# Attention branch with five seven-product quads in each pass, and one right factor formed ahead

## The chip, the cores and the metric

The kernel runs on one core of a Trainium2 chip. Its engines each work through an own stream of instructions: TensorE (PE: matmuls, and PEld: the loads of the stationary operand), VectorE (DVE), ScalarE (ACT), GpSimd (POOL), and SyncE (SP), which here only issues transfers. Sixteen DMA engines move data between HBM and the core's memory (SBUF). The metric is the device time of one launch in microseconds; the median of several runs is given, and a profile shows one execution in detail.

## What is computed

One layer that mixes dilated attention with a state-space scan, for 256 rows of width 2048, in float32. Cut to what matters here:

```python
hn = rms_norm(x, norm_w)
q, k, v, z_a, z_s, xbc, dt_raw, g_a, g_s = split(hn @ w_in)
...
o_a = o_a.reshape(b, s, ATTN_WIDTH) * silu(z_a)
y = rms_norm(y * silu(z_s), ssm_norm_w)
merged = sigmoid(g_a) * (o_a @ w_attn_branch) + sigmoid(g_s) * (y @ w_ssm_branch)
return rms_norm(x + merged @ w_out, final_norm_w)
```

The part that is changed is `o_a @ w_attn_branch`, a product of 256x2048 by 2048x2048 ("the attention branch").

## The kernel before

**Weights and units.** All weights lie in HBM as `wall`, an array of units of 128x1024 floats (512 KB), in the order in which they are used; `FIRST` gives each matrix's first unit. `load` (L263) fetches a unit into one of five tiles of a ring (`stream`, tag `w`, `W_BUFS = 5`). Float32 products are made from split operands: `unit` (L269) lets ScalarE round a unit to `h` (L278) and VectorE form the rest `l = w - h` (L279), each in one of four tiles (`H_BUFS = 4`). A product is then a triple of matmuls (`triple`, L483): left-high by h, left-high by l, left-low by h, lines L484 to L486.

**Stages, in order of time.** Scan stage (groups of the state-space part, with the x and z_s projections), the SSM branch, v, a loop over 16 heads (`q`, `k`, `za` projections, scores, mix), the attention gates `ga`, the attention branch `attn`, the output product `out`. The planner orders the instructions of each engine by a simulated timeline and by priorities; the order of the transfers on SP's queue comes with it.

**Passes and quads.** The products ga, attn and out run as two passes of 1024 columns each (c = 0 and c = 2), in `gemm_pair` (L469). A pass goes through eight quads; a quad is two blocks of 128 rows of the weights by two half-widths of 512 columns, for two halves of the 256 rows of the left side. A plain quad takes 2 x 2 x 2 products. A quad listed in `S_QUADS` takes seven, by Winograd's form of Strassen's product: it loads the four blocks of the weights (`wa` holds b11 and b21, unit n + 1 holds b12 and b22), forms T (two half-widths, from `b12 - b11` and `b22 - that`) and U = `wa` minus T's right half, splits four right factors (`ha/la`, `hc/lc`, `ht/lt`, `hu/lu`, by `part`, L550), and multiplies them with left factors; four of these are sums of blocks of the left side (`turn_x`, L450), made once and kept for both passes. The products that are shared go to four banks of their own (`prods`); `fold` (L585) adds them up at the end of a pass, and `attend` (L1146) then adds the plain sums and merges with the gates (L1143, L1144).

**Work done ahead.** T is formed ahead of time for the quads in `SUMS_ATT`: `sum_jobs` (L244) hangs a `get` behind a unit of the loop over the heads (two loads to a place in `th_a`, each behind a one-column copy on POOL, L249 and L250), and an `add` three units later (`SUM_LAG`): two half-width subtractions on VectorE (L254, L255) into a result place that itself waits for a POOL copy (L253), and a `spill` (L242) of 512 KB to HBM. The job frames are the same in the scan stage (`SUMS_SSM`). In the pass, T is loaded back (L533) along with b22 (L534); where `room` names places for these they take no tile of the ring. The left factors of o are made in `mix` behind every second head (`keep_left`, L425), spilled, and fetched on POOL's queue behind units named by `O_BEHIND` (L1115), into one buffer of the pool `xk` and four of `xl`, which until then hold the left factors of x.

**The branch before.** `S_QUADS` has (2, 4, 6) for pass 0 and (2, 4, 5, 6) for pass 2; the passes' orders of quads are in `A_ORDERS` (L41).

Of the kernel before, what the change touches and what calls it, by code (L numbers as in the profile page):

```python
# [24 lines left out]
UNIT = 1024  # L25
# [14 lines left out]
GS_BEFORE = {0: (0, 1), 4: (2,)}  # L40
A_ORDERS = {0: (0, 1, 2, 4, 3, 6, 5, 7), 2: (0, 2, 1, 4, 3, 5, 6, 7)}  # L41
V_ORDERS = {0: (0, 2, 4, 1, 3, 5, 6, 7), 2: (0, 2, 1, 4, 3, 5, 6, 7)}
# [9 lines left out]
    ("v", 0): (2, 3, 4, 5, 6), ("v", 2): (2, 4, 5, 6), ("ga", 0): (2, 3, 4, 5, 6), ("ga", 2): (2, 3, 4, 5, 6),  # L52
    ("attn", 0): (2, 4, 6), ("attn", 2): (2, 4, 5, 6), ("out", 0): (3, 5), ("out", 2): (3, 5),
}
# [4 lines left out]
SX_X = (2, 4, 3, 5, 6)  # L59
O_BEHIND = 3, 14, 15, 17  # L60
SUMS_ATT = [(t, q) for t in [(n, c) for n in ("ga", "attn", "out") for c in (0, 2)] for q in S_QUADS[t]]
ATT_QUADS = sorted({*S_QUADS[("attn", 0)], *S_QUADS[("attn", 2)]})
IN_PLACE = {"ssm": [(0, 12), (2, 12)]}
# [3 lines left out]
SUM_LAG = 3  # L67
# [58 lines left out]
FIRST = {}  # L126
# [72 lines left out]
def hybrid_block(ctx: ExitStack, tc: tile.TileContext, wall, xt, x, pk_d, cst_d, fw_d, out):  # L199
    nc = tc.nc  # L200
# [29 lines left out]
    on_unit = {}  # L230
    presum, lefts = {}, {}
    ssm_pool = []

    def behind_unit(n, f):
        on_unit.setdefault(n, []).append(f)
# [4 lines left out]
    def spill(kept, key, name, src, shape):  # L240
        kept[key] = dram.tile([P, *shape], F32, name=name, tag=name)
        nc.sync.dma_start(kept[key], src)  # L242

    def sum_jobs(jobs, units, places):  # L244

        def get(tag, q, t, b11, behind):
            n = FIRST[tag] + 2 * q
            for dst, src in ((t, wall[n + 1]), (b11, wall[n, :, :512])):
                gp.tensor_copy(dst[:, 0:1], behind)  # L249
                nc.sync.dma_start(dst, src)  # L250

        def add(tag, q, t, b11, res, behind):
            gp.tensor_copy(res[:, 0:1], behind)  # L253
            ve.tensor_tensor(res[:, :512], t[:, :512], b11, ALU.subtract)  # L254
            ve.tensor_tensor(res[:, 512:], t[:, 512:], res[:, :512], ALU.subtract)  # L255
            spill(presum, (tag, q), f"t_{tag[0]}{tag[1]}_{q}", res, [UNIT])

        for n, ((tag, q), u) in enumerate(zip(jobs, units)):
            t, b11, res = places[n % len(places)]
            behind_unit(u, lambda behind, a=(tag, q, t, b11): get(*a, behind))  # L260
            behind_unit(u + SUM_LAG, lambda behind, a=(tag, q, t, b11, res): add(*a, behind))

# [206 lines left out]
    def gemm_pair(tag, x_of, n_kt, sxs, swap, extra={}, close=1, order=None, room={}, tail=None):  # L469
# [22 lines left out]
        for at, q in enumerate(order):  # L492
# [29 lines left out]
            def place(kind):  # L522
                if not room.get(kind):
                    t = ring(f"{kind}{n}")
                    return t[:, 512:] if kind == "wc" else t
                seats[kind] = seats.get(kind, -1) + 1
                return room[kind][seats[kind] % len(room[kind])]

            wa = ring(f"wa{n}")
            nc.sync.dma_start(wa, wall[n])  # L530
            if made:
                wt, wc = place("wt"), place("wc")
                nc.sync.dma_start(wt, presum[tag, q])  # L533
                nc.sync.dma_start(wc, wall[n + 1, :, 512:])  # L534
            else:
                wt = ring(f"wb{n}")
                wc = wt[:, 512:]
                nc.sync.dma_start(wt, wall[n + 1])

            def hl(where, suffix, tags, bufs):  # L540
# [14 lines left out]
            with tc.high_priority(L_AHEAD):  # L555
                if not made:
                    ve.tensor_tensor(wt[:, :512], wt[:, :512], wa[:, :512], ALU.subtract)
                ha, la = hl(stream, "a", "hl", H_BUFS)
                part(wa, ha, la)
                hc, lc = hl(stream, "c", "hl", H_BUFS)  # L560
                part(wc, hc[:, :512], lc[:, :512])
                if not made:
                    ve.tensor_tensor(wt[:, 512:], wt[:, 512:], wt[:, :512], ALU.subtract)
                t2 = wt[:, 512:].unsqueeze(1).to_broadcast([P, 2, 512])
                ve.tensor_tensor(two(wa), two(wa), t2, ALU.subtract)
                ht, lt = pair_of("t")
                part(wt, ht, lt)
                hu, lu = pair_of("u")
                part(wa, hu, lu)
            sx = sxs[q]  # L570
# [121 lines left out]
    with tc.tile_pool(name="ssm", bufs=2) as sp:  # L692
# [212 lines left out]
        for c in GS_BEFORE[0]:  # L905
# [6 lines left out]
            SUMS_SSM, [FIRST[("B", g)] + n for g in range(1, 7) for n in SUM_UNITS],  # L912
            [(sums_at[:, 0], sums_at[:, 2, :512], sums_at[:, 1])],
        )
# [129 lines left out]
    with tc.tile_pool(name="att", bufs=2) as ap:  # L1044
# [33 lines left out]
        def mix(h, pT, za):  # L1078
# [204 lines left out]
```

## Time and profile before

| | |
|---|---|
| median of 3 runs | 1381.36 us (1379.6 to 1382.22) |
| the profiled execution | 1379.87 us, its span 1378.0 us |
| HBM read, written | 316.97 MB, 29.82 MB |
| loop over the heads | about 820 to 1115 us |
| attention gates | about 1116 to 1202 us |
| attention branch | 1196.8 to 1284 us |
| output product and end | from there to 1378 us |

A line of the groups names the source line, the engine, the operation, what is written from what (buffer numbers left out), the shape, the count, then busy time, mean ns of one, and the idle time in front of them with what ended it. A line of the waits names who waited for whom, the microseconds in total, how often, and the longest. A line of the stretches has its bounds, its length, the busy time of PE, PEld, DVE, ACT and POOL with counts, the granted clock, the DMA engines' busy share, and GB/s. A line of the DMA issues ends with the median microseconds from issue to landing. The stages overlap a little, since the planner lets matmuls of neighbouring quads interleave.

### The profile page before, as it was taken

Reading aid. Unit: us, or ns where it says so; the run is one execution under the profiler, and the core shown is the slowest. Engines: PE = TensorE matmul, PEld = TensorE weight load, DVE = VectorE, ACT = ScalarE, POOL = GpSimd, SP = SyncE. Lnnn points to the kernel's source line nnn. Section 1 sums busy time; section 2 is a strip of 40 time slices with the busy share of each in tenths; the row PEclk is TensorE's granted clock in tenths of the full one; section 3 lists DMA queues with packets and bytes.
Section 4 is the critical chain, followed back from the end, with each engine's and each line's share of the span. In section 5 each row is a group of like instructions: output and inputs, shape, how many; then the busy total and the mean of one; then the engine's idle time right before and its main releaser. Section 6 shows DMA issues by size and latency. Waiting matters only on the chain.

```text
span 1378.0 us, 20734 instructions
## 1 busy us (share of the span) xinstructions
PE 1366.8 (99%) x7260; PEld 1164.8 (85%) x7260; DVE 1177.0 (85%) x1763; ACT 840.0 (61%) x1310; POOL 161.7 (12%) x238
## 2 busy tenths in 40 slices
PE   9999999999999999999999999999999999999997
PEld 7888888888888888888888888888888888888886
DVE  6898899898899888788989888777877789988897
ACT  7655777675667676666565554454444557655564
POOL 2301211101020100010001001211211000400112
PEclk9999999999999999999999999999999999999999
DMA  9767878778787867578677568888889757875773
GB/s 342 237 190 237 298 267 286 262 244 288 248 277 237 298 203 220 174 242 277 228 261 270 211 215 316 306 275 280 306 298 302 230 163 267 291 244 173 246 273 122
DMA packets 106520, 348.15 MB, mean 253 GB/s; under 512 B 11888, under 2 KB 14256, under 8 KB 106416
## 3 DMA queue, kind: packets, MB, share of 16 engines
q1 hardware_dynamic: 104400, 340.67, 74.0%
q10 hardware_dynamic: 1440, 4.06, 0.8%
q0 software_dynamic: 576, 2.10, 0.4%
q8 instruction: 57, 0.93, 0.3%
q14 instruction: 47, 0.39, 0.1%
HBM read 316.97 MB, written 29.82 MB: 252 GB/s over the span
## 4 chain that ended last, share of the span: by engine, by line
PE 98%; DMA 0%; DVE 0%; ACT 0%; issue 0%; SPq 0%; POOL 0%; POOLq 0%; DVEq 0%
PE ps_xs L333 8%; PE ps_zs L333 8%; PE ps_k L333 4%; PE ps_za L333 4%; PE ps_q L333 4%; PE ps_zs L339 4%; PE ps_xs L339 4%; PE ps_ssm L485 3%; PE ps_ssm L486 3%; PE ps_ssm L484 3%; PE ps_q L339 2%; PE ps_za L339 2%; PE ps_k L339 2%; PE ps_gs L421 2%; PE ps_gs L422 2%; PE ps_gs L420 2%
## 5 line engine op out<-in xcount | busy, mean ns | idle before, releaser
L278 ACT ACTIVATE h<-w 128x1024 fp32r<-128x1024 f32 (+1 forms) x394 | 410.0, 1048 | 306.0 <-issue 73.7
L279 DVE TENSOR_TENSOR l<-w,h 128x1024 fp32r<-128x1024 f32 (+1 forms) x394 | 474.0, 1209 | 111.1 <-ACT h L278 106.9
L333 PE MATMUL ps_zs<-XT,h 128*128 128x512 f32 x496 | 172.0, 393 | 0.0
L333 PE MATMUL ps_xs<-XT,h 128*128 128x512 f32 x496 | 171.6, 393 | 0.0
L339 PE MATMUL ps_zs<-XT,l 128*128 128x256 f32 x496 | 134.6, 279 | 0.0
L339 PE MATMUL ps_xs<-XT,l 128*128 128x256 f32 x496 | 133.7, 277 | 0.0
L333 PEld LDWEIGHTS ps_xs<-XT,h 128*128 128x128 f32 x496 | 91.3, 188 | 19.4
L333 PEld LDWEIGHTS ps_zs<-XT,h 128*128 128x128 f32 x496 | 91.3, 188 | 18.9
L339 PEld LDWEIGHTS ps_zs<-XT,l 128*128 128x128 f32 x496 | 93.3, 188 | 2.1
L339 PEld LDWEIGHTS ps_xs<-XT,l 128*128 128x128 f32 x496 | 93.2, 188 | 2.1
L333 PE MATMUL ps_q<-XT,h 128*128 128x512 f32 x256 | 91.1, 404 | 0.0
L333 PE MATMUL ps_k<-XT,h 128*128 128x512 f32 x256 | 88.6, 395 | 0.0
L333 PE MATMUL ps_za<-XT,h 128*128 128x512 f32 x256 | 88.4, 394 | 0.0
L551 ACT ACTIVATE ha<-wa 128x1024 fp32r<-128x1024 f32 x45 | 47.5, 1056 | 45.9 <-PE ps_ssm L486 10.0
L339 PE MATMUL ps_q<-XT,l 128*128 128x256 f32 x256 | 68.4, 278 | 0.0
L339 PE MATMUL ps_k<-XT,l 128*128 128x256 f32 x256 | 68.4, 277 | 0.0
L339 PE MATMUL ps_za<-XT,l 128*128 128x256 f32 x256 | 68.4, 277 | 0.0
L552 DVE TENSOR_TENSOR la<-wa,ha 128x1024 fp32r<-128x1024 f32 x45 | 54.8, 1218 | 8.4 <-ACT ha L551 8.3
L552 DVE TENSOR_TENSOR ltu<-wa,htu 128x1024 fp32r<-128x1024 f32 x40 | 48.7, 1219 | 10.8 <-ACT htu L551 10.8
L793 ACT ACTIVATE gt<-acb,acT 128x128 f32<-128x128 f32 x128 | 44.1, 390 | 22.2 <-DMA acb<-acum_d 21.9
L333 PEld LDWEIGHTS ps_k<-XT,h 128*128 128x128 f32 x256 | 47.0, 188 | 9.9
L333 PEld LDWEIGHTS ps_q<-XT,h 128*128 128x128 f32 x256 | 47.1, 188 | 9.7
(691 smaller groups left out, 3347.8 us busy)
## 6 DMA issues: line engine op xcount, KB each, us to landing
w<-in_wall SPq DMA_DIRECT2D x390, 512.0 KB, 4.8
wa<-in_wall SPq DMA_DIRECT2D x45, 512.0 KB, 4.7
th_a<-in_wall SPq DMA_DIRECT2D x21, 512.0 KB, 4.7
sums_at<-in_wall SPq DMA_DIRECT2D x18, 512.0 KB, 5.0
acb<-acum_d SPq DMA_DIRECT2D x32, 256.0 KB, 3.8
t_ssm<-sums_at SPq DMA_DIRECT2D x13, 512.0 KB, 4.3
wt<-t_ssm SPq DMA_DIRECT2D x13, 512.0 KB, 4.7
th_a<-in_wall SPq DMA_DIRECT2D x21, 256.0 KB, 5.4
```

The source lines that it names most:

```text
L278: ac.activation(h[:, a:b], w[:, a:b], AF.Copy)
L279: ve.tensor_tensor(l[:, a:b], w[:, a:b], h[:, a:b].bitcast(F32), ALU.subtract)
L333: high = pe.matmul(acc, h[:, kk, :], xs_of(kt), start=(kt == 0), stop=False)
L339: low = pe.matmul(acc[:, S:], l[:, kk, :], xs_of(kt)[:, :S], start=False, stop=(kt == KT - 1))
L420: pe.matmul(accs[i], xh, h[:, kk], start=(kt == 0), stop=False)
L421: pe.matmul(accs[i], xh, l[:, kk], start=False, stop=False)
L484: pe.matmul(acc, xh, h, start=start, stop=False)
L485: pe.matmul(acc, xh, l, start=False, stop=False)
L486: pe.matmul(acc, xl, h, start=False, stop=stop)
L551: ac.activation(h, src, AF.Copy)
L552: ve.tensor_tensor(l, src, h.bitcast(F32), ALU.subtract)
L793: ac.activation(g4[:, n, b], acb[:, j, b // 2 * P : b // 2 * P + P], AF.Relu, scale=-1.0, bias=sc[:, h : h + 1],)
```

## The change

Both passes of the branch get the same five seven-product quads, 2 to 6, and the same order. A fifth left factor of o (quad 3) is made, spilled and fetched. For quads 3 to 6 of both passes U is formed ahead too: the job loads all of `wa`, forms T in place of its second operand, then U in place of `wa`, and spills both; in the pass U is loaded by a transfer of its own (alternately to a new tile `room_u` and to a tile of the ring) and `wa` stays as it is. Jobs now work in place, with no third place and no POOL copy at the add; the scan stage's jobs use two places by turns instead of one. There are 24 jobs in the loop over the heads in place of 21, spaced 17/5 units in place of 15/4.

```diff
-A_ORDERS = {0: (0, 1, 2, 4, 3, 6, 5, 7), 2: (0, 2, 1, 4, 3, 5, 6, 7)}
+A_ORDERS = {0: (0, 2, 3, 1, 4, 5, 6, 7), 2: (0, 2, 3, 1, 4, 5, 6, 7)}
...
-    ("attn", 0): (2, 4, 6), ("attn", 2): (2, 4, 5, 6), ("out", 0): (3, 5), ("out", 2): (3, 5),
+    ("attn", 0): (2, 3, 4, 5, 6), ("attn", 2): (2, 3, 4, 5, 6), ("out", 0): (3, 5), ("out", 2): (3, 5),
...
-O_BEHIND = 3, 14, 15, 17
+U_QUADS = 3, 4, 5, 6
+O_BEHIND = 3, 3, 14, 15, 17
...
+SUMS_U = {(t, q) for t, q in SUMS_ATT if t[0] == "attn" and q in U_QUADS}
...
-        def get(tag, q, t, b11, behind):
+        def get(tag, q, t, b, behind):
             n = FIRST[tag] + 2 * q
-            for dst, src in ((t, wall[n + 1]), (b11, wall[n, :, :512])):
+            b = b if (tag, q) in SUMS_U else b[:, :512]
+            for dst, src in ((t, wall[n + 1]), (b, wall[n, :, : b.shape[-1]])):
...
-        def add(tag, q, t, b11, res, behind):
-            gp.tensor_copy(res[:, 0:1], behind)
-            ve.tensor_tensor(res[:, :512], t[:, :512], b11, ALU.subtract)
-            ve.tensor_tensor(res[:, 512:], t[:, 512:], res[:, :512], ALU.subtract)
-            spill(presum, (tag, q), f"t_{tag[0]}{tag[1]}_{q}", res, [UNIT])
+        def add(tag, q, t, b, behind):
+            name = f"{tag[0]}{tag[1]}_{q}"
+            ve.tensor_tensor(t[:, :512], t[:, :512], b[:, :512], ALU.subtract)
+            ve.tensor_tensor(t[:, 512:], t[:, 512:], t[:, :512], ALU.subtract)
+            spill(presum, (tag, q), f"t_{name}", t, [UNIT])
+            if (tag, q) in SUMS_U:
+                t2 = t[:, 512:].unsqueeze(1).to_broadcast([P, 2, 512])
+                two = b.rearrange("p (k m) -> p k m", k=2)
+                ve.tensor_tensor(two, two, t2, ALU.subtract)
+                spill(u_sums, (tag, q), f"u_{name}", b, [UNIT])
...
+            if (tag, q) in u_sums:
+                wu = place("wu")
+                nc.sync.dma_start(wu, u_sums[tag, q])
...
-                t2 = wt[:, 512:].unsqueeze(1).to_broadcast([P, 2, 512])
-                ve.tensor_tensor(two(wa), two(wa), t2, ALU.subtract)
+                if (tag, q) not in u_sums:
+                    wu = wa
+                    t2 = wt[:, 512:].unsqueeze(1).to_broadcast([P, 2, 512])
+                    ve.tensor_tensor(two(wa), two(wa), t2, ALU.subtract)
...
-                part(wa, hu, lu)
+                part(wu, hu, lu)
...
-            [(sums_at[:, 0], sums_at[:, 2, :512], sums_at[:, 1])],
+            [(sums_at[:, n], sums_at[:, 2, n * 512 : n * 512 + 512]) for n in range(2)],
...
-            SUMS_ATT, [FIRST[("q", 0)] + 3 + n * 15 // 4 for n in range(len(SUMS_ATT))],
-            [
-                (th_a[:, i, :UNIT], th_a[:, 1, UNIT + 512 * i : UNIT + 512 * i + 512], th_a[:, 0, UNIT:])
-                for i in range(2)
-            ],
+            SUMS_ATT, [FIRST[("q", 0)] + 3 + n * 17 // 5 for n in range(len(SUMS_ATT))],
+            [(th_a[:, i, :UNIT], th_a[:, i, UNIT:]) for i in range(2)],
...
-        room = {"wt": [fin[:, i, UNIT:] for i in range(2)], "wc": [fin[:, i, :512] for i in range(2)]}
+        room = {
+            "wt": [fin[:, i, UNIT:] for i in range(2)], "wc": [fin[:, i, :512] for i in range(2)],
+            "wu": [fp.tile([P, UNIT], F32, name="room_u", tag="room_u", bufs=1), None],
+        }
```

More of the change, by code (lines that the diff above doesn't have):

```diff
@@ L230, in hybrid_block @@
     on_unit = {}
-    presum, lefts = {}, {}
+    presum, u_sums, lefts = {}, {}, {}
     ssm_pool = []
@@ L244, in sum_jobs @@
     def sum_jobs(jobs, units, places):
-        def get(tag, q, t, b11, behind):
+        def get(tag, q, t, b, behind):
             n = FIRST[tag] + 2 * q
-            for dst, src in ((t, wall[n + 1]), (b11, wall[n, :, :512])):
+            b = b if (tag, q) in SUMS_U else b[:, :512]
+            for dst, src in ((t, wall[n + 1]), (b, wall[n, :, : b.shape[-1]])):
                 gp.tensor_copy(dst[:, 0:1], behind)
                 nc.sync.dma_start(dst, src)
-        def add(tag, q, t, b11, res, behind):
-            gp.tensor_copy(res[:, 0:1], behind)
-            ve.tensor_tensor(res[:, :512], t[:, :512], b11, ALU.subtract)
-            ve.tensor_tensor(res[:, 512:], t[:, 512:], res[:, :512], ALU.subtract)
-            spill(presum, (tag, q), f"t_{tag[0]}{tag[1]}_{q}", res, [UNIT])
+        def add(tag, q, t, b, behind):
[8 more added lines that the diff above has]
+                spill(u_sums, (tag, q), f"u_{name}", b, [UNIT])
         for n, ((tag, q), u) in enumerate(zip(jobs, units)):
-            t, b11, res = places[n % len(places)]
-            behind_unit(u, lambda behind, a=(tag, q, t, b11): get(*a, behind))
-            behind_unit(u + SUM_LAG, lambda behind, a=(tag, q, t, b11, res): add(*a, behind))
+            t, b = places[n % len(places)]
+            behind_unit(u, lambda behind, a=(tag, q, t, b): get(*a, behind))
+            behind_unit(u + SUM_LAG, lambda behind, a=(tag, q, t, b): add(*a, behind))
     def load(n, cuts=(0, UNIT)):
@@ L522, in place @@
             def place(kind):
-                if not room.get(kind):
+                seats[kind] = seats.get(kind, -1) + 1
+                spots = room.get(kind) or [None]
+                t = spots[seats[kind] % len(spots)]
+                if t is None:
                     t = ring(f"{kind}{n}")
                     return t[:, 512:] if kind == "wc" else t
-                seats[kind] = seats.get(kind, -1) + 1
-                return room[kind][seats[kind] % len(room[kind])]
+                return t
             wa = ring(f"wa{n}")
```

## The prediction, made before the run

> **What bounds the kernel now.** I read the page from the top: span, engine shares, the 40 slices, the chain that ended last.
>
> ```profile
> span 1378.0 us, 20734 instructions
> PE 1366.8 (99%) x7260; PEld 1164.8 (85%) x7260; DVE 1177.0 (85%) x1763; ACT 840.0 (61%) x1310; POOL 161.7 (12%) x238
> PEclk9999999999999999999999999999999999999999
> PE 98%; DMA 0%; DVE 0%; ACT 0%; issue 0%; SPq 0%; POOL 0%; POOLq 0%; DVEq 0%
> ```
>
> TensorE is busy 99% of the span at a full granted clock, and the chain is 98% TensorE. Ends of matmuls are modelled, so I asked two more views whether this is real work: TensorE's waits (the whole answer is two lines, both in the first ten microseconds), and the chain in order of time inside the attention branch.
>
> ```profile
> PE warm L630 <- DVE ssq L627: 1.4, 1, 1.4
> PE ps_first L385 <- ACT h L278: 1.4, 2, 1.1
> 1216.71 0.68 PE ps_attn L484 x3
> 1220.56 0.68 PE ps_attn L484 x3
> 1270.46 0.68 PE pp_attn L484 x3
> ```
>
> Three 128x512 matmuls take 0.68 us, early and late in the branch, whichever operand they use: 0.68 / 3 = 0.227 us each. So time is the number of matmuls, and everything else has to arrive before its turn.
>
> **The change, part by part. Matmuls.** A plain quad issues 2 x 2 x 2 products of three matmuls, 24; a seven-product quad issues 21. Before, the branch has 3 + 4 of them, after 5 + 5: three more, 9 matmuls fewer, 9 x 0.227 = **2.04 us off the path**. Nothing behind the branch is shortened or lengthened, so the end of the kernel moves with it.
>
> The Trainium skill ("Perfetto Trace Analysis", Identifying the Most-Contended Engine) says that matmul busy time is a poor measure and weight-load time a better one; that reads 85% here, and at the 188 ns of a weight load the nine would be worth about 1.7 us. The 0.68 us per three, without a wait, speaks for the larger number; the sign is the same.
>
> **VectorE and ScalarE in the branch.** The groups of VectorE by form, and ScalarE's, in the two passes:
>
> ```profile
> L279 DVE TENSOR_TENSOR l<-w,h 128x1024 fp32r<-128x1024 f32 x18 | 21.6, 1218 | 3.8 <-ACT h L278 3.8
> L552 DVE TENSOR_TENSOR ltu<-wa,htu 128x1024 fp32r<-128x1024 f32 x7 | 8.5, 1220 | 0.2 <-ACT htu L551 0.2
> L565 DVE TENSOR_TENSOR wa<-wa,fin 128x1024 f32<-128x1024 f32 x7 | 8.5, 1217 | 0.0
> L552 DVE TENSOR_TENSOR lc<-fin,hc 128x512 fp32r<-128x512 f32 x7 | 4.8, 684 | 0.9 <-ACT hc L551 0.9
> L1143 DVE SCALAR_TENSOR_TENSOR th_a<-th_a,fin 128x512 f32<-128x512 f32 x4 | 2.6, 680 | 0.0
> L278 ACT ACTIVATE h<-w 128x1024 fp32r<-128x1024 f32 x20 | 20.4, 1052 | 6.5 <-PE ps_attn L486 5.2 <-PE ps_ga L486 1.2
> L551 ACT ACTIVATE hc<-fin 128x512 fp32r<-128x512 f32 x7 | 4.4, 622 | 7.8 <-DMA fin<-in_wall 4.5 <-PE ps_attn L486 3.3
> ```
>
> A plain quad costs VectorE 2 x 1.22 = 2.44 us; a seven-product one three wide splits, a narrow one and the subtraction of U, 4 x 1.22 + 0.68 = 5.56; with U summed ahead, 4.34. Before: 7 x 5.56 + 9 x 2.44 = 60.9 us; after: 2 x 5.56 + 8 x 4.34 + 6 x 2.44 = 60.5 us. So the branch asks VectorE for no more. ScalarE's part grows by 3 x (3 x 1.05 + 0.62 - 2 x 1.05) = 5 us, which its idle time takes:
>
> ```profile
> 1196.80:1240.60 43.80, 43.80 (x195) 36.25 (x194) 38.87 (x44) 25.59 (x30) 0.48 (x1) 1.00 0.76 259
> 1240.60:1285.00 44.40, 44.40 (x205) 36.83 (x204) 39.70 (x50) 25.62 (x33) 3.16 (x1) 1.00 0.59 189
> 820.00:1115.00 295.00, 295.00 (x1714) 258.92 (x1714) 224.65 (x424) 146.07 (x223) 43.57 (x63) 1.00 0.83 282
> ```
>
> (Columns: stretch, length, busy PE, PEld, DVE, ACT, POOL, clock, DMA share, GB/s.) ScalarE is busy 51 of 88 us there. Loads of the branch grow by 8 U of 0.52 MB and 3 x 0.26 MB, 5.0 MB; 259 x 43.8 + 189 x 44.4 is 19.7 MB, so 24.7 MB in 86 us is 287 GB/s, about what the third row already carries with TensorE 295 of 295 us busy. Cost taken: 0.
>
> **What moves ahead, into the loop over the heads (third row).** Three more summing jobs of two half-width subtractions, eight subtractions of U, one more left factor of o.
>
> ```profile
> L254 DVE TENSOR_TENSOR th_a<-th_a 128x512 f32<-128x512 f32 x21 | 14.5, 691 | 5.7 <-POOL th_a L253 3.5 <-DMA th_a<-in_wall 1.0
> L459 DVE TENSOR_TENSOR sxt_o<-sxt_o x4: 281/282/284, 976.5 to 1120.7; 128x128 f32<-128x128 f32 x4
> L288 DVE TENSOR_TENSOR sxt_o<-sxt_o x4: 681/684/686, 982.1 to 1125.1; 128x512 fp32r<-128x512 f32 x4
> ```
>
> VectorE: 3 x 2 x 0.69 + 8 x 1.22 + (0.68 + 4 x 0.28 + 0.68) = 16.4 us, from 225 to 241 of 295 us. U out of place has no row of its own; L565 is the same form. The 21 POOL copies at L253 go; they hold nothing that ends last. Cost 0 while the 54 us of idle VectorE last. The job frames of the SSM stages change the same way (in place, two places by turns): fewer POOL copies, a place reused at every second job rather than each one; TensorE has no wait there to win or lose.
>
> **The transfers of those jobs** are the one place where I see a resource come near its end. The DMA view and the stages:
>
> ```profile
> w<-in_wall SPq DMA_DIRECT2D x36, 512.0 KB, 5.4
> t_attn<-th_a SPq DMA_DIRECT2D x7, 512.0 KB, 6.1
> 930.00:1040.00 110.00, 110.00 (x645) 96.81 (x644) 83.92 (x164) 54.42 (x86) 19.21 (x28) 1.00 0.87 296
> 836.00:848.00 12.00, 12.00 (x71) 10.52 (x70) 8.00 (x11) 5.45 (x8) 1.12 (x4) 1.00 0.96 360
> 1195.00:1204.00 9.00, 9.00 (x41) 7.46 (x40) 7.65 (x11) 5.15 (x7) 1.69 (x4) 1.00 0.97 378
> 951.00:953.50 2.50, 2.50 (x18) 2.28 (x17) 2.17 (x4) 1.82 (x5) 0.00 (x0) 1.00 0.89 169
> ```
>
> 36 weight loads in 110 us: 3.06 us per unit. The jobs of the branch come every 17/5 = 3.4 units (before 15/4), ten of them in 34 units = 104 us. In these: 34 x 0.52 = 17.8 MB of weights; 2 jobs load 0.79 MB, 8 load 1.05 MB: 10.0 MB; 2 + 16 spills and some 2 of left factors: 10.5 MB. Together 38.3 MB in 104 us, **368 GB/s, where 296 fill 87%**. Per full share the first stretch gives 296 / 0.87 = 340 GB/s, the second 375, the third (loads alone) 390; 38.3 MB are 113, 102 or 98 us. The last row, just behind a spill's issue, is the worst: 0.52 MB at 169 GB/s and share 0.89 is 2.8 us; if each spill cost that, 27.8 / 0.39 + 20 x 2.8 = 127 us. So the stretch is 6 us long to 23 us short. Against it stand buffers: five weight tiles (5 x 3.06 = 15.3 us around the ring, less 5.4 landing, 1.06 and 1.22 for the split: 7.6 us to spare) and four split tiles (4 x 3.06, less the one in use and the same split: 6.9 us). Up to 14.5 us late, TensorE sees nothing. The row nearest to a busy queue is the second, 375 GB/s: cost taken 0, ends 0 and 23 - 14.5 = 8.5 us.
>
> The Trainium skill differs with itself here: "DMA: Bandwidth & Descriptors" (Where 436 GB/s comes from) lets about 358 GB/s bind a transfer from HBM, by which the stretch is 3 us short; "Perfetto Trace Analysis" (Roofline) lets one core alone go to some 430, by which it fits. The 378 GB/s measured over 9 us agrees with the second.
>
> **The waits added.** On SP's queue a second spill stands behind VectorE's subtraction of U, 1.2 us more per job; weight loads queue behind it, and the 7.6 us above are their slack. A place's next loads wait for both spills: load at a unit, sum 3 units (9.2 us) later, some 2.6 us of sums, 6.1 us of landing: 17.9 us against the 2 x 3.4 x 3.06 = 20.8 us at which the place comes round. On POOL the second left factor fetched behind unit 3 of the last gate pass waits for a buffer of x; queued behind it are only the other three fetches, wanted later.
>
> **The new order** sets quads 2 and 3 early in both passes and leaves one plain quad, not two, behind the last seven-product one of pass 1 (6, 7 against 6, 5, 7). There VectorE folds, adds and merges: 16 x 0.68 = 10.9 us. From the end of quad 6 to quad 2 of pass 2 VectorE owed, before, 3 x 2.44 + 10.9 + 5.56 = 23.8 us beside 3 x 5.44 + 4.76 = 21.1 us of TensorE; after, 2 x 2.44 + 10.9 + 5.56 = 21.3 beside 15.6. It falls behind by 5.7 us, not 2.7: 3.0 us worse. How near it was:
>
> ```profile
> 1247.05 0.68 DVE L552 TENSOR_TENSOR lc<-fin,hc 128x512 fp32r<-128x512 f32 x1
> 1249.08 0.48 PE L485 MATMUL ps_attn<-lc,sx_o 128*128 128x512 f32 x1
> 1158.00:1200.00 42.00, 41.98 (x187) 34.45 (x185) 39.94 (x43) 28.29 (x34) 14.72 (x8) 1.00 0.83 282
> ```
>
> lc is done at 1247.73 and used at 1249.08, 1.35 us later. So the bounds are 0 and 3.0 - 1.35 = 1.65 us. The gate passes already run the order 6, 7 | 0, 2 with five such quads and U subtracted on the spot, VectorE 95% busy, and TensorE is idle 0.02 us (last row); but their fold and adds are 5.5 us, not 10.9. Merges can slip behind the splits, so I take 0.
>
> **Sum**, against the profiled execution's own 1379.87 us (span 1378.0 and 1.87 around it): 1379.87 - 2.04 = 1377.83. The median of the runs is 1381.36, 1.49 above it; on that footing **1379.3 us**, 0.15% faster. About 0.2% (2.8 us) is what a measurement can tell from no change, so the forecast lies within it.
>
> **Rivals.** *The DMA queue becomes the bound* in the ten jobs of the branch: weights come late, the ring runs dry, TensorE waits. For it: 368 GB/s asked, and the 169 GB/s row. Against it: ScalarE waits for a weight only once in the heads' stage now, and the 12 us at 360 GB/s hold two spills (both rows below, from the waits and from the DMA issues of those 12 us). It decides once the stretch is over 14.5 us short, that is 118 us for 104; at the worst row it costs 8.5 us: 1379.3 + 8.5 = 1387.8, slower.
>
> ```profile
> ACT h L278 <- DMA w<-in_wall: 0.2, 1, 0.2
> t_ga<-th_a SPq DMA_DIRECT2D x2, 512.0 KB, 6.8
> ```
>
> *VectorE is late at the seam of the passes*: 1.65 us of the 2.04 go, 1381.0, no change.
>
> *The rest lands, but the run is better than the sum*: the spread of the runs shown is 1379.6 to 1382.22, so a true 2.0 us can read as 2.8 or more: 1378.5 or less.
>
> **How the numbers follow.** Forecast 0.62 (of it one part in five reads as faster by over 0.2%: 0.13); DMA queue 0.22 (slower when over 4.8 us are lost, 0.16, else no change); seam 0.13 (no change, 0.02 of it slower, if both add up); a stall that I haven't seen 0.03, slower. Faster 0.13, within 0.2% 0.66, slower 0.21. Range: 1379.3 less the spread of the runs below their median, 2, to the DMA rival's full price: 1377.3 to 1387.5.
>
> **What would show it.** 7251 matmuls, not 7260; TensorE's waits still two lines; between the first and last matmul of the branch about 2 us less. DMA rival: share 0.95 and over in the slices from 936 to 1040 us, ScalarE's h waiting for w by microseconds, TensorE for h at L333. Seam: TensorE waiting for l or lc near 1245 us. If the heads' stage keeps its 295 us and the gain is still not 2 us, the count of matmuls was the wrong measure.

## The result, and the profile after

The changed kernel takes **1401.37 us** (median of 5 runs, 1398.49 to 1405.06) against 1381.36 (1379.6 to 1382.48): 1.0149 times as long, interval 1.0136 to 1.0162. The forecast was 1379.3, and the range ended at 1387.5. First the head of the page of after: span, engines, granted clock and the chain that ended last.

```profile
span 1397.9 us, 20746 instructions
PE 1375.5 (98%) x7251; PEld 1166.0 (83%) x7251; DVE 1186.6 (85%) x1784; ACT 842.8 (60%) x1317; POOL 113.1 (8%) x207
PEclk9999999999999999999999999999999999999999
PE 88%; DMA 4%; DVE 4%; ACT 2%; issue 2%; POOL 1%; SPq 0%; POOLq 0%; DVEq 0%; ACTq 0%
```

The nine matmuls are gone (7251), and yet TensorE is busy for longer and the chain leaves it for 12% of the span, most of it for transfers, VectorE and ScalarE. To find where, I took the starts of the same matmuls in both traces and cut the time at the first matmul of the SSM branch, of q, of ga, and at the last one (all in us; some 8 us behind the last matmul are in no row). Stages are always those of the one profiled execution of a kernel, whose time can differ from the median of its runs:

| stage | before | after |
|---|---|---|
| to the SSM branch (the scan stage) | 574.2 | 584.1 |
| SSM branch and v | 247.5 | 247.6 |
| loop over the heads | 294.7 | 297.2 |
| gates, attention branch, output | 252.9 | 260.7 |

The last row should have become 250.9 (252.9 less the 2.04 of nine matmuls). So 9.9 us are lost in the scan stage, which the prediction passed over in one sentence, 2.5 in the heads' loop, and 9.8 behind it.

**Scan stage and heads.** The waits of after, first in a window of the scan stage (150 to 325 us), then in the heads' loop (820 to 1130); columns: who waited for whom, total, times, longest.

```profile
DVE sums_at L257 <- DMA sums_at<-in_wall: 13.7, 6, 3.8
PE ps_xs L347 <- DVE l L287: 3.1, 2, 1.6
PE ps_gs L429 <- DVE l L287: 1.4, 2, 1.3
...
DVE th_a L257 <- DMA th_a<-in_wall: 29.9, 14, 4.5
```

Before, the first window has no wait of VectorE for a load; POOL stood there instead, and in the heads' loop VectorE waited 1.0 us for loads (answers for before):

```profile
POOL sums_at L253 <- issue: 29.8, 5, 11.6
...
POOL th_a L253 <- ACT h L278: 124.0, 16, 9.7
DVE th_a L254 <- DMA th_a<-in_wall: 1.0, 1, 1.0
```

One stall in full, from the timelines of after (SP's queue, VectorE, TensorE; start, length):

```profile
239.43 0.81 SPq L253 DMA_DIRECT2D sums_at<-in_wall  x2
...
242.61 0.42 DVE L403 SCALAR_TENSOR_TENSOR zh<-ps_zs,lo_z 128x256 f32<-128x256 f32 x1
244.00 0.69 DVE L257 TENSOR_TENSOR sums_at<-sums_at 128x512 f32<-128x512 f32 x1 [0.96 <-DMA sums_at<-in_wall]
244.60 1.75 DVE L818 TENSOR_TENSOR gt<-gt,cb 128x1536 f32<-128x1536 f32 x1
246.28 1.22 DVE L287 TENSOR_TENSOR l<-w,h 128x1024 fp32r<-128x1024 f32 x1
...
250.94 1.22 DVE L287 TENSOR_TENSOR l<-w,h 128x1024 fp32r<-128x1024 f32 x1
...
252.21 0.39 PE L347 MATMUL ps_xs<-XT,l 128*128 128x256 f32 x1 [1.52 <-DVE l L287]
```

The reader is to see this: a job's loads are issued at 239.43, VectorE comes to its subtraction 3.6 us later, the load lands another 0.96 us after that, and the splits behind it start late until TensorE stands 1.52 us for an l, eight microseconds further on. The job of before at the same place of VectorE's stream, behind the same zh (timelines of before):

```profile
232.92 0.81 SPq L250 DMA_DIRECT2D sums_at<-in_wall  x2
235.73 0.41 DVE L395 SCALAR_TENSOR_TENSOR zh<-ps_zs,lo_z 128x256 f32<-128x256 f32 x1
241.69 1.36 POOL L253 COPY sums_at<-h 128x1 f32<-128x1 f32 x1 [8.68 <-issue]
241.79 1.22 DVE L279 TENSOR_TENSOR l<-w,h 128x1024 fp32r<-128x1024 f32 x1
243.09 0.69 DVE L254 TENSOR_TENSOR sums_at<-sums_at 128x512 f32<-128x512 f32 x1
```

There the subtraction starts 10.2 us after the issue of its loads, without a wait, and behind the split l. From zh to this l it is 6.1 us (235.73 to 241.79), in after 8.3 (242.61 to 250.94): the 0.96 us of waiting and the job's own two subtractions of 0.7 now stand in front of it.

**The branch.** The stretches of after round the seam of the passes (columns as before), TensorE's two waits there, and VectorE in between:

```profile
1240.00:1262.00 22.00, 20.93 (x94) 17.08 (x92) 18.08 (x21) 10.27 (x12) 0.00 (x0) 1.00 0.70 260
1262.00:1275.00 13.00, 10.08 (x39) 7.42 (x40) 12.90 (x19) 8.62 (x12) 0.00 (x0) 0.74 0.60 189
...
1260.46 1.22 DVE L580 TENSOR_TENSOR wa<-wa,fin 128x1024 f32<-128x1024 f32 x1
1261.60 1.28 DVE L1169 TENSOR_TENSOR fin<-ps_attn,fin 128x512 f32<-128x512 f32 x2
1262.79 1.29 DVE L1158 SCALAR_TENSOR_TENSOR th_a<-th_a,fin 128x512 f32<-128x512 f32 x2
1264.00 1.22 DVE L565 TENSOR_TENSOR ltu<-wa,htu 128x1024 fp32r<-128x1024 f32 x1
...
1262.89 0.58 PE L492 MATMUL ps_attn<-htu,oaTa 128*128 128x512 f32 x1 [1.95 <-ACT htu L564]
1265.27 0.80 PE L493 MATMUL ps_attn<-ltu,oaTa 128*128 128x512 f32 x1 [1.80 <-DVE ltu L565]
```

VectorE is busy 12.90 of 13 us; quad 2 of pass 2, whose U is not formed ahead, gets its ltu behind two sums and two merges of pass 0. And the granted clock is 0.74 there.

### The profile page after: what moved, and what is told of

Read it like the earlier page. It is cut to its first block, busy times and chain, and to the rows that moved or that the text cites. A ratio compares the mean times of both kernels' runs of the same rounds, so it can differ in the third digit from the quotient of the medians.

```text
span 1397.9 us, 20746 instructions
## 1 busy us (share of the span) xinstructions
PE 1375.5 (98%) x7251; PEld 1166.0 (83%) x7251; DVE 1186.6 (85%) x1784; ACT 842.8 (60%) x1317; POOL 113.1 (8%) x207
## 4 chain that ended last, share of the span: by engine, by line
PE 88%; DMA 4%; DVE 4%; ACT 2%; issue 2%; POOL 1%; SPq 0%; POOLq 0%; DVEq 0%; ACTq 0%
PE ps_zs L341 6%; PE ps_xs L341 6%; PE ps_za L341 4%; PE ps_k L341 4%; PE ps_q L341 4%; PE ps_zs L347 3%; PE ps_xs L347 3%; PE ps_ssm L493 3%; PE ps_ssm L494 3%; PE ps_ssm L492 3%; PE ps_q L347 2%; PE ps_k L347 2%; PE ps_za L347 2%; PE ps_gs L429 2%; PE ps_gs L430 2%; PE ps_gs L428 2%
## 5 line engine op out<-in xcount | busy, mean ns | idle before, releaser
L286 ACT ACTIVATE h<-w 128x1024 fp32r<-128x1024 f32 (+1 forms) x388 | 403.0, 1046 | 249.9 <-issue 52.8
L287 DVE TENSOR_TENSOR l<-w,h 128x1024 fp32r<-128x1024 f32 (+1 forms) x388 | 467.4, 1210 | 65.1 <-ACT h L286 61.6
L564 ACT ACTIVATE ha<-wa 128x1024 fp32r<-128x1024 f32 x48 | 50.7, 1055 | 52.6 <-DMA wa<-in_wall 12.5
L565 DVE TENSOR_TENSOR la<-wa,ha 128x1024 fp32r<-128x1024 f32 x48 | 58.6, 1222 | 14.3 <-ACT ha L564 14.0
L341 PEld LDWEIGHTS ps_za<-XT,h 128*128 128x128 f32 x256 | 46.9, 188 | 10.0
```

Source lines behind the costliest of these rows:

```text
L286: ac.activation(h[:, a:b], w[:, a:b], AF.Copy)
L287: ve.tensor_tensor(l[:, a:b], w[:, a:b], h[:, a:b].bitcast(F32), ALU.subtract)
L341: high = pe.matmul(acc, h[:, kk, :], xs_of(kt), start=(kt == 0), stop=False)
L564: ac.activation(h, src, AF.Copy)
L565: ve.tensor_tensor(l, src, h.bitcast(F32), ALU.subtract)
```

## Experiments

Two theories at the start. **Gate**: the POOL copy in front of the subtractions (before, L253) was no cost but an order: VectorE could not reach them until the h of three units later existed, and by then the loads had landed. Rivals: **places** (it is the work in place, and the two places by turns, that move the transfers) and **bandwidth** (the larger jobs fill the queue). For the branch: **VectorE** is the bound at the seam; rivals **place** (b22's place is freed only by the merges) and **loads**. All stage times below are cut as above, in one profiled execution each; us is the median of the runs. The kernel before, run beside them, took 1380.3 to 1380.6 us.

| run | us | scan | SSM, v | heads | rest |
|---|---|---|---|---|---|
| gate_back | 1387.59 | 576.1 | 247.4 | 294.7 | 259.0 |
| before_no_gate | 1399.70 | 584.0 | 247.5 | 305.2 | 253.5 |
| two_plain_at_seam | 1400.89 | 583.5 | 248.2 | 300.7 | 256.2 |
| gate_and_order | 1384.92 | 576.0 | 247.4 | 294.7 | 257.1 |
| old_scan_frame | 1383.35 | 575.3 | 247.8 | 294.7 | 257.2 |
| u_of_quad_2_too | 1387.85 | 577.0 | 247.5 | 295.6 | 258.8 |
| old_scan_frame_u2 | 1386.37 | 577.3 | 247.4 | 295.6 | 257.7 |
| b22_own_place | 1388.57 | 576.9 | 248.0 | 294.7 | 260.9 |
| b22_free_at_seam_2 | 1386.27 | 574.9 | 247.6 | 294.8 | 259.2 |
| four_plain_b22_free_2 | 1385.09 | 574.5 | 247.4 | 294.7 | 257.0 |
| three_plain_at_seam | 1385.55 | 575.5 | 247.5 | 294.8 | 259.0 |
| five_quads_no_u | 1392.39 | 574.1 | 247.4 | 294.7 | 264.2 |
| u_ahead_only | 1381.89 | 574.8 | 247.5 | 294.7 | 253.5 |
| eight_quads | 1385.39 | 576.2 | 248.3 | 294.7 | 256.3 |
| nine_quads | 1382.89 | 574.3 | 247.7 | 294.7 | 256.1 |

**1. The gate put back** into the changed kernel, in place, so that no third buffer is needed (`zero` is one new column):

```diff
         def add(tag, q, t, b, behind):
             name = f"{tag[0]}{tag[1]}_{q}"
+            gp.tensor_tensor(zero, behind, behind, ALU.subtract)
+            gp.tensor_tensor(t[:, 0:1], t[:, 0:1], zero, ALU.add)
             ve.tensor_tensor(t[:, :512], t[:, :512], b[:, :512], ALU.subtract)
```

> The changed kernel with one thing back: VectorE's sums of a job wait again for POOL, and POOL for the unit three further on (POOL adds a zero, formed from that unit's h, to the first column of T's place). Theory gate: the POOL copy that went with the change was what held the sums back until their loads had landed; without it the planner sets them as early as its own timeline lets the loads land, and VectorE, in order, waits on the real transfer with all splits behind it. Then the 9.9 us lost in the scan stage and the 2.5 us in the loop over the heads come back and VectorE's waits for th_a and sums_at loads go from 44 us to a few: 1401.4 - 12.4, about 1389 us. Rival places: it is the work in place, and two places by turns, that moves the transfers; then 1401 us stays and the waits with it. Rival bandwidth: the scan stage comes back, the heads' 2.5 us stay: 1391.5 us.

It took 1387.59 us: 13.8 of the 20 are back, and the rival of the places falls, since they stayed as they were. By stages 8.0 us are back in the scan stage, 2.5 in the heads' loop and 1.7 in the rest. The heads' loop is at 294.7, exactly before's, with the larger jobs and their transfers in it (a stretch of it in gate_back, columns as before):

```profile
930.00:1040.00 110.00, 110.00 (x645) 96.82 (x644) 91.96 (x176) 55.18 (x86) 24.59 (x40) 1.00 0.95 354
```

The DMA engines are busy 95% of it and TensorE 110.00 of 110 us, so bandwidth falls as a rival too. VectorE's waits for the jobs' loads are gone from its answer; what is left there are 5.7 us for POOL's gate in the heads, which no matmul feels.

**2. The gate taken out of the kernel before**, and nothing else:

```diff
         def add(tag, q, t, b11, res, behind):
-            gp.tensor_copy(res[:, 0:1], behind)
             ve.tensor_tensor(res[:, :512], t[:, :512], b11, ALU.subtract)
```

> The kernel before without the POOL copy at the sums (L253), all else as it was: one place in the scan stage, a third place for the result, three and four quads. Theory gate: the scan stage loses about the same 10 us (position of the first matmul of the SSM branch 584 instead of 574 us), VectorE waits for sums_at loads by 10 us and more; 1388 to 1392 us. Rival places: the copy has nothing to do with it, 1380 us and no wait.

1399.70 us (1.0134 times before, 1.0101 to 1.0166), 9.8 us lost in the scan stage, 10.5 in the heads, 0.6 behind them. The scan stage came as expected; the loss in the heads, and with it the total, was not foreseen. The waits of this kernel over the whole span:

```profile
DVE th_a L253 <- DMA th_a<-in_wall: 61.2, 20, 5.5
DVE sums_at L253 <- DMA sums_at<-in_wall: 24.9, 11, 5.4
```

One line of one column, on an engine that is 12% busy, is worth 19 us, in a kernel that has nothing else of the change. That settles the heads and, with the 8.0 us of gate_back, most of the scan stage.

**3, 4. Two plain quads more at the seam**, without and with the gate:

```diff
-A_ORDERS = {0: (0, 2, 3, 1, 4, 5, 6, 7), 2: (0, 2, 3, 1, 4, 5, 6, 7)}
+A_ORDERS = {0: (0, 2, 3, 4, 5, 6, 1, 7), 2: (0, 1, 2, 3, 4, 5, 6, 7)}
```

> The changed kernel with another order of quads: pass 0 (0, 2, 3, 4, 5, 6, 1, 7), pass 2 (0, 1, 2, 3, 4, 5, 6, 7), so four plain quads and not two lie between the last seven-product quad of pass 0 and the first of pass 2. Theory seam: the 7.2 us that TensorE idles from 1260 to 1270 us are VectorE's fold, adds and merges falling together with the splits of quad 2; with 2 x 5.44 us more of TensorE's own work between them the idle time goes, 1401.4 - 7 = 1394 us. Rival loads: the branch is short of transfers (U, T, b22 come late); then idle time of some 7 us stays, wherever in the branch.

> Both edits together. If they are two causes in two places, the gains add: 1401.4 - 12.4 - 7.2 = 1382 us, and with the 2.7 us at the seam from the gates to the branch gone too, 1379 us. If one only uncovers the other, less comes back than the sum of the two alone.

Without the gate nothing can be read from the total, 1400.89: the heads, which the edit doesn't name, lost 6.0 us in place of 2.5. With it, 1384.92 against gate_back's 1387.59. The rest went from 259.0 to 257.1: the order of quads is worth about 2 us in it, and some 6 to the goal of 250.9 stay. The gains of 1 and 3 were expected to add up to 1382 or less; they didn't.

**5, 6. U of quad 2 ahead as well**, and b22 in places that no merge holds (the halves of room_u, U then in the ring), each alone on gate_back:

```diff
-U_QUADS = 3, 4, 5, 6
+U_QUADS = 2, 3, 4, 5, 6
```

```diff
-            "wt": [fin[:, i, UNIT:] for i in range(2)], "wc": [fin[:, i, :512] for i in range(2)],
-            "wu": [fp.tile([P, UNIT], F32, name="room_u", tag="room_u", bufs=1), None],
+            "wt": [fin[:, i, UNIT:] for i in range(2)], "wc": [room_u[:, i * 512 : i * 512 + 512] for i in range(2)],
```

> gate_back, with U of quad 2 summed ahead as well in both passes (ten U in place of eight); order and places of the branch as in the change. Theory: the seam between the passes is bound by VectorE, which was busy without a gap there and whose subtraction of U for quad 2 of pass 2 stood in the chain in front of TensorE's wait (1.22 us, then ScalarE's htu, then ltu). Then the loss at the seam shrinks by at least those 1.2 us, by about 2.4 if the half-clock phase goes too: branch shift over before +5.4 to +6.6 where gate_back had +6.1 of loss and ended at 7.8, so total 1385 to 1386.4. Rival (places: b22's place is freed only by the merges, and loads at the seam come late): the chain behind hc and lc stays as it is, nothing is gained, 1387.6 and the 4 long waits near 1250 us unchanged. Rival (transfers of the jobs): two more U to load and spill make the heads' stage longer than before's, loss over 0.3 us there.

> gate_back, with the two places of b22 taken from the new tile room_u (its two halves) and not from fin, where a merge frees them; every U of the branch takes a tile of the ring instead. Rival (places): the wait of hc for its load (3.9 us in the changed kernel) goes, and the loss at the seam falls by about what stands behind it, 1 to 2 us: total near 1386, no DMA fin wait of hc. Theory (VectorE): the first two waits of the seam (for htu and ltu, 2.1 us each in gate_back) stand ahead of hc and stay; at most 0.5 us is gained; and with U in the ring the weights of the plain quads come later, so it can lose as much.

Neither pays: 258.8 and 260.9 against 259.0. In the first the waits for htu and ltu are gone, but TensorE stands 4.0 us in two waits (the longer 3.2) before the transposes (L1154), which want the last merges: VectorE had the same fold, sums and merges to do, and only who waits for it changed. In the second the waits at the seam are halved, and others come at the tail of the gates, where U now takes tiles from the ring of the weights.

**7, 8. The scan stage's old job frame** (one place, a result place, the copy), with the order of 4; then with U of quad 2 too:

```diff
-            [(sums_at[:, n], sums_at[:, 2, n * 512 : n * 512 + 512]) for n in range(2)],
+            [(sums_at[:, 0], sums_at[:, 2, :512], sums_at[:, 1])],
```

> gate_and_order, with the summing jobs of the scan stage in the old frame: one place, a result place of its own, the POOL copy in front of the subtractions; the loop over the heads keeps the new frame with the gate. Theory: the scan stage's remaining shift of +1.9 us comes from the two places used by turns (the next loads can start earlier and gather with other transfers): it goes, 1384.9 - 1.9 = 1383.0. Rival: it comes from something else (the smaller head start of the whole program, two POOL operations where there was one): the shift stays at +1.9, total 1384.9.

> old_scan_frame with U of quad 2 summed ahead too. Theory (VectorE bounds the seam): with two plain quads behind quad 6 and 1.22 us less in front of quad 2, VectorE is less behind: seam loss from about 2 us to under 1; total 0.5 to 1.5 below old_scan_frame, 1381.5 to 1382.5. Rival (places, loads): no change against old_scan_frame; and if the two more U to load and spill fill the queue, a wait for w near 1190 us grows from 1.6 us.

1383.35, 1.6 below gate_and_order, about as the theory had it; but that is luck, if anything: the runs of the two overlap (1381.99 to 1385.67 and 1383.15 to 1386.77), the two profiled executions took 1384.94 and 1385.08, and the scan stage, 575.3, is only 0.7 shorter. With U of quad 2 (nothing of the scan stage differs) it is 577.3, and the rest, 257.7 against 257.2, has gained nothing. So a spread of up to 3 us in the scan stage belongs to no edit that I tried. In the traces it is no wait: over stretches of 20 to 50 us the step from one matmul of ps_xs by h to the next by l is 0.235 to 0.242 us in place of 0.230 to 0.233. Why is open, and stage times of the scan that differ by less than 3 us say nothing here.

**9 to 12. More at the seam.** Three plain quads (both passes in the order 0 to 7), on old_scan_frame; then, apart from it, b22 of pass 2's first two seven-product quads in room_u, on gate_back (two plain quads) and on old_scan_frame (four):

```diff
-A_ORDERS = {0: (0, 2, 3, 1, 4, 5, 6, 7), 2: (0, 2, 3, 1, 4, 5, 6, 7)}
+A_ORDERS = {0: (0, 1, 2, 3, 4, 5, 6, 7), 2: (0, 1, 2, 3, 4, 5, 6, 7)}
```

```diff
+            "wc": [*(fin[:, i, :512] for i in (0, 1, 0, 1, 0)), room_u[:, :512], room_u[:, 512:], *(fin[:, i, :512] for i in (0, 1, 0))],
+            "wu": [room_u, None, room_u, None, None, None, room_u, None],
+        }
+        seats.update(wc=-1)
```

> old_scan_frame, with both passes in the order 0 to 7: plain quads 0 and 1 stand first in both passes, so three plain quads (7, 0, 1) lie between the last and the first seven-product quad at the seam (four in old_scan_frame, two in the change), and the gate passes' tail is followed by two plain quads as in the kernel before. Theory (loads at the tail of the gate passes): the 2.6 us idle between 1187 and 1203 us go, since quad 2's and 3's loads (wa, T, b22, U) no longer crowd w there; seam idle 1 to 3 us (one plain quad fewer than old_scan_frame): 1381 to 1383. Rival (VectorE and places at the seam decide): seam idle back to 4 to 6 us, 1384 to 1387.

> gate_back, order of the change, b22 of the first two seven-product quads of pass 2 in the two halves of room_u, the counter of places started anew at the branch so that the places fall where they are meant to. Rival (places): hc of quad 2 of pass 2 waits for no load, the waits behind it at the seam go, idle of the seam falls from 6.5 us by 2 to 4 us and the half-clock phase with it: 1383.5 to 1385.5. Theory (VectorE, busy without a gap with fold, sums and merges and with quad 2's splits): TensorE's waits for htu and ltu stay, at most 1 us gained: 1386.5 to 1387.6.

> old_scan_frame (four plain quads at the seam) with the same places of b22. Its own seam idle is 1.1 us behind waits for merges and for ltu: at most 1 us to win, 1382.4 to 1383.4; if U in the ring brings weights late, up to 1 us lost.

Three runs with b22 in room_u failed as experiments (b22_free_at_seam 1388.92, three_plain_b22_free 1390.68, four_plain_b22_free 1386.20): without the last line of the diff the counter of places runs on from earlier stages, U of a quad lands on its own b22 before that is split, and they test nothing. With it, b22_free_at_seam_2 leaves the rest at 259.2 against gate_back's 259.0, and four_plain_b22_free_2 at 257.0 against 257.2; three_plain_at_seam has 259.0, no less than gate_back with two plain quads. But the rest is a sum of two places. Cut once more, at the 101st matmul of the branch in each trace (in the middle of pass 0, behind the gates and ahead of the seam), it reads:

| run | plain quads at the seam | from ga to there | from there to the last matmul |
|---|---|---|---|
| before | 3 | 105.3 | 147.6 (goal 145.6) |
| gate_back | 2 | 106.2 | 152.8 |
| b22_free_at_seam_2 | 2 | 108.2 | 151.0 |
| b22_own_place | 2 | 110.5 | 150.4 |
| three_plain_at_seam | 3 | 107.4 | 151.5 |
| old_scan_frame | 4 | 108.8 | 148.4 |
| four_plain_b22_free_2 | 4 | 106.5 | 150.5 |

So the order with four plain quads wins 4.4 us at the seam (152.8 to 148.4), and 2.6 of them are lost in front of it; three plain quads fall between. With b22 free the seam is 1.8 and 2.4 us shorter where two plain quads stand there, and 2.1 longer where four do. With one trace each, it is not settled whether the place has a part of some 2 us in the seam of the change. VectorE at the seam, gate_back first, then b22_free_at_seam_2 (stretches):

```profile
1248.00:1251.00 3.00, 0.88 (x4) 0.33 (x2) 3.00 (x5) 1.06 (x1) 0.00 (x0) 1.00 0.25 72
1251.00:1258.00 7.00, 5.05 (x17) 3.58 (x18) 6.90 (x10) 3.29 (x5) 0.00 (x0) 0.51 0.61 196
```

```profile
1248.00:1251.00 3.00, 2.53 (x14) 1.77 (x12) 3.00 (x5) 2.54 (x4) 0.00 (x0) 1.00 0.00 0
1251.00:1258.00 7.00, 5.17 (x19) 3.32 (x19) 7.00 (x10) 1.94 (x2) 0.00 (x0) 1.00 0.84 284
```

VectorE is busy 9.9 and 10.0 of 10 us, with b22 free or not.

**13, 14. The change taken apart.** The kernel before with five quads in each pass, the fifth left factor, the order of 4 and the jobs every 17/5 units, but U formed in the pass (its edit is shown); and old_scan_frame with before's quads, orders, left factors and spacing, so that of the change only U ahead is left:

```diff
-    ("attn", 0): (2, 4, 6), ("attn", 2): (2, 4, 5, 6), ("out", 0): (3, 5), ("out", 2): (3, 5),
+    ("attn", 0): (2, 3, 4, 5, 6), ("attn", 2): (2, 3, 4, 5, 6), ("out", 0): (3, 5), ("out", 2): (3, 5),
...
-O_BEHIND = 3, 14, 15, 17
+O_BEHIND = 3, 3, 14, 15, 17
```

> The kernel before with its own job frames (three places, POOL copy) and five seven-product quads in each pass, the order with four plain quads at the seam, the fifth left factor, jobs every 17/5 units: U is formed in the pass for all. 7251 matmuls. Theory (VectorE's slack in the branch is what the change spends, and U ahead pays for it): VectorE has 8 x 1.22 = 9.8 us more in the branch than old_scan_frame, most of it has slack, but quads 3 to 6 stand in a row: 3 to 6 us more idle than old_scan_frame within the passes, less 1 to 2 us that the loads of U cost at the gate passes' tail: 1383 to 1388. Rival (U ahead does not pay: its loads and spills cost as much as they save): at or below old_scan_frame, 1379 to 1383.

> The change's job frames with the gate back and the old frame in the scan stage, but the quads, orders, left factors and spacing of the kernel before (three and four seven-product quads): of the change only U ahead (five of seven quads) is left. 7260 matmuls. Theory (the extra seven-product quads in a row at the seam cost, not U): within 1 us of before, 1379.5 to 1381.5, the waits between 1187 and 1203 us gone. Rival (the loads of U and the larger jobs crowd the queue): the 2.6 us idle at the gate passes' tail stay, 1382 to 1384.

1392.39, above what either side expected, and 1381.89. U ahead costs no more than 0.6 us in the rest (253.5 against 252.9), and TensorE waits there once, 0.22 us in the gates; the five quads cost 11.3 (264.2), and U ahead gives 7.0 of them back (257.2, old_scan_frame). VectorE in the branch, five_quads_no_u, old_scan_frame and u_ahead_only in this order (stretches):

```profile
1240.00:1292.00 52.00, 46.65 (x201) 36.28 (x200) 48.98 (x60) 29.03 (x36) 0.68 (x1) 0.97 0.63 205
```

```profile
1240.00:1284.00 44.00, 42.85 (x193) 33.86 (x192) 43.23 (x55) 27.97 (x35) 0.18 (x1) 1.00 0.76 256
```

```profile
1239.00:1284.00 45.00, 45.00 (x208) 37.38 (x207) 38.75 (x50) 25.24 (x32) 2.47 (x1) 1.00 0.68 225
```

VectorE is 94% and 98% busy over the whole second half of the branch in the first two, 86% in the third, where TensorE has no gap.

**15, 16. One and two of the three quads alone**, on u_ahead_only, with the fifth left factor and the jobs every 17/5 units, which these quads need or bring along:

```diff
-    ("attn", 0): (2, 4, 6), ("attn", 2): (2, 4, 5, 6), ("out", 0): (3, 5), ("out", 2): (3, 5),
+    ("attn", 0): (2, 3, 4, 6), ("attn", 2): (2, 3, 4, 5, 6), ("out", 0): (3, 5), ("out", 2): (3, 5),
```

(The edit of nine_quads; eight_quads has pass 2 as it was.)

> u_ahead_only with one more seven-product quad: quad 3 of pass 0, which stands between plain or finished quads in the order of the kernel before (0, 1, 2, 4, 3, 6, 5, 7); pass 2 as before; U ahead for quads 3 to 6. The seam keeps its three plain quads. 7257 matmuls. Theory (U ahead is free, and a seven-product quad costs nothing where VectorE has room): u_ahead_only less 3 x 0.227 = 0.7 us, 1381.2, 0 to 1 us above before. Rival (any row of seven-product quads, here 2, 4, 3, 6, overloads VectorE): 1383 to 1385.

> eight_quads with quad 3 of pass 2 as well, in the order (0, 2, 1, 4, 3, 5, 6, 7): nine seven-product quads, one fewer than the change, 7254 matmuls, U ahead for quads 3 to 6. Theory (only the seam was short of VectorE): 1.36 us below u_ahead_only, 1380.5, the same as before; TensorE without waits in pass 0 and at the seam. Rival (the row 4, 3, 5, 6 of pass 2 overloads VectorE or brings loads late near its end): 1 to 3 us idle between 1270 and 1290 us, 1381.5 to 1384.

1385.39 and 1382.89; neither theory came true, and where the rival of nine_quads looked, between 1270 and 1290 us, there is one wait of 0.5 us. The rest is 256.3 and 256.1 where 252.8 and 252.1 were to be had from 253.5; the totals differ by more because of the scan stage (576.2 and 574.3). The largest wait of both is not in the branch: near 1190 us, at the tail of the gate passes, TensorE waits 1.7 and 1.6 us for an h. What differs there from u_ahead_only is the fifth left factor (the added quads come later in their passes, and the jobs are over by then). The fetches on POOL and ScalarE's h after them, u_ahead_only first, then eight_quads (timelines):

```profile
1175.36 0.80 POOL L455 DMA_DIRECT2D sx_o<-sxd_o  x1 [0.31 <-POOL sx_o L454]
1193.29 0.55 POOL L455 DMA_DIRECT2D sx_o<-sxd_o  x1 [0.31 <-POOL sx_o L454]
...
1187.39 1.06 ACT L292 ACTIVATE h<-w 128x1024 fp32r<-128x1024 f32 x1 [1.75 <-DMA w<-in_wall]
```

```profile
1177.75 0.80 POOL L455 DMA_DIRECT2D sx_o<-sxd_o  x1 [0.31 <-POOL sx_o L454]
1185.37 0.55 POOL L455 DMA_DIRECT2D sx_o<-sxd_o  x1 [0.31 <-POOL sx_o L454]
...
1192.95 1.06 ACT L292 ACTIVATE h<-w 128x1024 fp32r<-128x1024 f32 x1 [4.94 <-DMA w<-in_wall]
```

A second 512 KB come at 1185.37, in the middle of the last weights of the gates; in u_ahead_only they come at 1193.29. The same wait (0.2 to 2.0 us) stands in all runs of the table with five left factors but old_scan_frame, five_quads_no_u, which loads no U, among them, and in none of the three kernels with four. In all of these the second fetch starts 19 to 22 us ahead of the last matmul of the gates. In old_scan_frame and in the change itself it starts 17.4 us ahead, and there the late weight is a later one: TensorE waits 0.96 and 0.85 us among the first matmuls of the branch. A run with the fifth fetch alone moved was not made, so this is a strong suspicion, not shown.

No version beat the kernel before; the nearest, u_ahead_only (1.0010 times before, 1.0000 to 1.0019), has all of its matmuls.

## Why the prediction was wrong

**The step that failed** is a sentence given as a price of nothing: "The 21 POOL copies at L253 go; they hold nothing that ends last. Cost 0", and for the scan stage "TensorE has no wait there to win or lose". I read the copies as work, on an engine with room, and looked for who waits for them (VectorE, 3.5 us). What they did was to hold VectorE's stream: with them, the subtractions stood behind a late h, without them behind a transfer of real length. Putting the gate back returns 10.5 us (8.0 of the 9.9 in the scan stage, all 2.5 in the heads), and taking it out of the kernel before costs 19. The 1.9 us of the scan stage that stay with the gate back lie within the spread of that stage, and their cause is open. The row was in the prediction: "5.7 <-POOL th_a L253 3.5 <-DMA th_a<-in_wall 1.0" names the gate and, right beside it, the load that it hides.

**The seam was a rival at 1.65 us; it is the second cause, mis-sized.** Gate_back has it nearly alone: 8.1 us in the rest against the goal, 7.2 of them behind the branch's 101st matmul. The working ("21.3 beside 15.6", 3.0 worse, margin 1.35) counted splits, fold, sums and merges, but took 0 because "Merges can slip behind the splits". They didn't: ltu came behind two sums and two merges (1264.00). The transposes of pass 0 too wait for the last merge, and the splits of those (four, 0.68 us each) weren't counted. Nor was it seen that one late split in a row that is already full is followed by the next. That VectorE is the bound there rests on its 12.90 of 13 us and on five_quads_no_u, where eight more subtractions of 1.22 us, 9.8 us, cost 7.0; what b22's place adds to it is open.

**"So the branch asks VectorE for no more"** (60.9 to 60.5 us) is right as a sum and misled as an argument: TensorE's time shrinks by 2 us, the work gathers behind five quads in a row, and the margin by place, not the sum, decided.

**Matmuls**: 7251, as said; the step of 0.227 us from one 128x512 matmul to the next is the same in after, so nine fewer are 2.04 us less of TensorE's own work; no run shows that gain by itself. The Trainium skill's weight-load measure ("Perfetto Trace Analysis", Identifying the Most-Contended Engine) reads 83% after, and tells neither of the stalls.

**Transfers of the jobs**: right. With the gate the heads' loop is 294.7 us, and the 354 GB/s of gate_back from 930 to 1040 us are near the 368 asked. The share of 0.95, named as a sign of the DMA rival, is there, and TensorE feels nothing.

**Waits on SP and POOL**: the second spill and the place coming round cost nothing. The second fetch on POOL "waits for a buffer of x; queued behind it are only the other three" looked at POOL's queue, but not at the transfer it starts: the suspected 0.2 to 2 us at the tail of the gates.

**Chances**: slower had 0.21, and no rival was about the gate. (The range ends at 1387.5, where the DMA rival's own sum gives 1387.8.) The signs named in advance did their work: TensorE waiting at the seam, and ScalarE's h for w not by much in the heads (one wait of 2.9 us in gate_back).

## What to carry to other kernels

An instruction that does no work may be the only thing that keeps an engine's stream from standing at a transfer: before a copy, a memset or a one-column write is priced at nothing, ask what becomes free to move when it is gone, and how long the thing behind it really takes. Cutting matmuls from a TensorE-bound stage did not pay here, where VectorE, which prepares the operands, was busy 94% to 98% of that very stretch; look at VectorE by stretches of ten microseconds, not by stage. And a transfer that is moved earlier, as the fetch of the fifth left factor suggests, is to be priced against what is landing at that moment, not against the queue it stands in.

## What was not expected of the hardware

The half clock at the seam: in gate_back TensorE stood 1.95 and 1.88 us with a single matmul in between, and from 1251 to 1258 us the granted clock was 0.51 (rows above); after shows the same with 0.74 over 13 us, which is (1 - 0.74) x 13 / 0.5 = 6.8 us at half speed. five_quads_no_u shows 0.75 from 1283.3 to 1290.0 us, right behind a gap of 2.54 us: 3.4 us at half speed. The Trainium skill ("TensorE: Matmul & The Clock Gate", What's actually happening) gives windows of about 3.4 us of activity; 6.8 is two of them and 3.4 one, and no single gap here was as long as one. b22_free_at_seam_2, with gaps of 0.47, 0.45 and 1.37 us, kept the full clock. Behind the 101st matmul it took 1.8 us less than gate_back (151.0 against 152.8), so the phase and b22's place together showed 1.8 us there, and what the phase alone cost is open.
